# RWKV and attention in a hybrid encoder layer: side products moved to other places of TensorE's order, the value projection first, the queries' low part in both partition halves

## Chip, cores and metric

One core of a Trainium2 chip runs the whole layer. The metric is the device time of one execution in microseconds (us), lower is better. Time before: 884.14 us, the median of 3 runs (883.92 to 884.91).

## What is computed

One encoder layer on x of 512 positions by 1024 channels, float32. The parts that the change touches, from the reference:

```python
# h = rms_norm(x); proj = h @ w_in, its columns go to four mixers A, B, C, D and four gates
# B: stick-breaking attention, 4 heads x 64; mask is kpos < qpos
z = einsum('bhqd,bhkd->bhqk', qi, kh) * scale
log_beta = log_sigmoid(z)
log_keep = where(mask, log_beta - z, 0.0)
suffix = cumsum(log_keep, axis=3, reverse=True) - log_keep
attn = where(mask, exp(log_beta + suffix), 0.0)
out = einsum('bhqk,bhkd->bhqd', attn, vh)
# C: RWKV-7, 4 heads x 64: S_t = S_{t-1} diag(w_t) + (S_{t-1} a_t) b_t^T + v_t k_t^T ; y_t = S_t r_t
# D: u * (causal 128x128 mixing of layer_norm(v)), with u, v = split(gelu(z))
merged = sum over the branches of sigmoid(gate_i) * (y_i @ out_i);  x = x + merged @ w_o
# then rms_norm, the gated FFN with a width-3 convolution (2816 hidden), and a last rms_norm
```

## The kernel before

**Products.** Every large product is made of triples: `mm3` (lines 168 to 172) issues three matmuls of 512 columns, hi·hi, hi·lo and lo·hi, since each float32 operand is split into a part `hi` in the matmul type fp32r and a remainder `lo` (`split`, lines 99 to 101: ScalarE casts hi at L100, VectorE subtracts at L101; in all other helpers that split, the same two lines show). A weight arrives in pieces of 256 KB on SyncE's queue, is split into `whi` and `wlo`, and is used by four triples; seven such pieces are held.

**Order.** TensorE's order is written by hand: it runs in program order of the code. All other engines get their order from a scheduler, and each then executes strictly in its order. After each triple `mm3` calls `tick()` (line 159), which advances side threads by one: "norm", "rw" (first RWKV half, later attention), "rw1" (second RWKV half) and "sg" (mixer D's tail). A thread is a generator, and its `yield n` waits n triples. The numbers n are the constants `YA` to `YH`, `Y1` and `YS` (lines 33 to 35), and these place the side products between the triples.

**The RWKV half** (`rwkv_half`, j = 0 and 1, two heads each) goes, in TensorE's order: the gate product with `g2` (L434), sums over a head's channels by a matmul with a block of ones (L416, via `head_sum`), 64-row instances against masks, and a triangular solve. For the solve VectorE forms inverses of 16x16 blocks, which go out to DRAM and come back as `Dc`, and from that `Dm` (L541). `all_inst` (L552) issues 16 products of 64x64 as one group; `P1` (Dm by AoT) comes `YC` triples after `AkV`, `T32` and `TT` (L566, L568) one step later, and L578 reads `T32`. After that come `GT`, `pC`, `pY` (L612 to L625), and six steps of the state scan (L639 on TensorE, L640 and L641 on VectorE), `YS` triples apart. Between head sums and scan VectorE also computes the normalised keys (L462 and on) from `y0`, which ScalarE makes with a logarithm and an exponential (L448, L449).

**Mixer D's tail** (`sg_tail`): gelu of four 128x512 blocks on ScalarE (L794), layer-norm statistics and twelve operations on VectorE (L810 to L812, three for each block), the causal mixing on TensorE (L817).

**Attention.** Queries, keys and values come from three products of 16 triples each, in this order. Per head (four: `j`, `hp`), with `own` the head's 64 partitions and `oth` the other 64: `kS[:, hp]` holds k_hi on `own` and k_lo on `oth`; `qS[:, hp]` holds q_hi on both; `qL` holds q_lo on `own` only. The scores take, for each of four key blocks `si` (512, 384, 256 and 128 columns wide), one product over 128 rows (L931: k_hi·q_hi + k_lo·q_hi), one over 64 rows (L932: k_hi·q_lo) and the mask (L933). This is called the z block below. Then, 1 triple later, ScalarE takes |z|, an exponential and a logarithm (L940 to L942), VectorE adds (L944), a split gives `spH`, `spL`, and `YE` = 15 triples later L952 takes the cumulative sums; ScalarE takes the exponential (L956), a split gives `aH`, `aL`, and `YF` = 5 triples later L964 multiplies with the values. The values were transposed at L908, directly after their product. ScalarE also computes the branch gates (L850, a sigmoid); it loads a function table (ACT_TABLE_LOAD) where the next function isn't in the one that is loaded.

Of the kernel before, what the change touches and what calls it, by code (L numbers as in the profile page):

```python
# [9 lines left out]
F32 = mybir.dt.float32  # L10
F32R = mybir.dt.float32r
# [4 lines left out]
P = 128  # L16
# [13 lines left out]
NWB = 9  # L30
NACT = 8

YA, YB, YC, YD, YE, YF, YG, YH = 6, 16, 32, 20, 15, 5, 11, 3
Y1 = 3
YS = 2
WN = 19
WN2 = 5
ND = 3
# [10 lines left out]
def hybrid_encoder_layer(  # L49
# [22 lines left out]
    def bank(tag="mm"):  # L72
        return psum.tile([P, 512], F32, tag=tag, name=tag, bufs=4)
# [55 lines left out]
    def col_unit(w, *cols, get=piece):  # L129

        n = 256 // len(cols)
        return [get(2, [(slice(n * i, n * i + n), w[:, 2 * h:2 * h + 2, c:c + n]) for i, c in enumerate(cols)]) for h in range(w.shape[1] // 2)]
# [10 lines left out]
    def spawn(thread, gen):  # L143
        threads.setdefault(thread, []).append([gen, 0])
# [194 lines left out]
    def gemm2(u):  # L339

        ps = [bank(), bank()]
        for ci, kt in [(ci, kt) for h in range(4) for ci in range(2) for kt in range(2 * h, 2 * h + 2)]:
            hi, lo = u[kt // 2]
            cs = slice(ci * P, (ci + 1) * P)
            mm3(ps[ci], hi[:, kt % 2, cs], lo[:, kt % 2, cs], hH[:, kt, :], hL[:, kt, :], kt == 0, kt == KT - 1)
        return ps
# [50 lines left out]
    def rwkv_half(j, lora, xg, zk, zr, zv):  # L397
# [31 lines left out]
        cs = t2("tF", "cs")  # L429
        vec.tensor_tensor_scan(out=cs, data0=scan_m.rearrange("p c t -> p (c t)"), data1=sg, initial=0.0, op0=ALU.mult, op1=ALU.add)  # L430
        head_sum = parts_of(sq)
        yield 3
        pg = bank("wk")
        pe.matmul(pg, lhsT=g2[:, cj], rhs=xg, start=True, stop=True)  # L434
        gT = t2("gT", bufs=2)
# [435 lines left out]
    apool, ast = open_pool("apool", "right")  # L871


    HS = [slice(0, 64), slice(64, P)]
    qS, qL, kS, vS = [], [], [], []

    def lo_of(out, src, hi):
        vec.tensor_tensor(out=out, in0=src, in1=hi.bitcast(F32), op=ALU.subtract)

    pss2 = gemm2(col_unit(w_in_v, SB0))  # L880
    for j in range(2):
        ps = pss2[j]
        qs = apool.tile([P, 2, T], F32R, tag="qS", name="qS", bufs=2)
        ql = apool.tile([P, T], F32R, tag="qL", name="qL", bufs=2)
        for hp in range(2):
            own, oth = HS[hp], HS[1 - hp]
            act.mul(qs[own, hp, :], ps[own, :], 0.125)
            act.mul(qs[oth, hp, :], ps[own, :], 0.125)
            vec.scalar_tensor_tensor(out=ql[own, :], in0=ps[own, :], scalar=0.125, in1=qs[own, hp, :].bitcast(F32), op0=ALU.mult, op1=ALU.subtract)
        qS.append(qs)  # L890
        qL.append(ql)
    pss2 = gemm2(col_unit(w_in_v, SB0 + 256))
    for j in range(2):
# [4 lines left out]
            act.copy(ks[own, hp, :], ps[own, :])  # L898
            lo_of(ks[oth, hp, :], ps[own, :], ks[own, hp, :])
        kS.append(ks)  # L900
    pss2 = gemm2(col_unit(w_in_v, SB0 + 512))
    for j in range(2):
        ps = pss2[j]
        v = apool.tile([P, T], F32, tag="vT", name="vT", bufs=2)
        act.copy(v, ps)
        pt = bank("wk")
        for s in range(4):
            pe.transpose(out=pt[:, s * P:(s + 1) * P], in_=v[:, s * P:(s + 1) * P], identity=ident)  # L908
        vs = apool.tile([P, 2, NT, P], F32R, tag="vS", name="vS", bufs=2)
        for hp in range(2):  # L910
            own, oth = HS[hp], HS[1 - hp]
            src = pt.rearrange("p (s c) -> p s c", s=4)[:, :, own]
            act.copy(vs[:, hp, :, own], src)
            lo_of(vs[:, hp, :, oth], src, vs[:, hp, :, own])
        vS.append(vs)

    OFF = [0, 512, 1024, 896]
    W = [512, 384, 256, 128]
    def attention():
        for j in range(2):  # L920
            yt = apool.tile([P, T], F32, tag="yt", name="yt", bufs=2)
            for hp in range(2):
                own, oth = HS[hp], HS[1 - hp]
                zb = [bank("wk"), bank("wk"), bank("wk")]

                def zreg(si, t0=0):
                    b, o = divmod(OFF[si], 512)
                    return zb[b][:, o + t0:o + W[si]]

                for si in range(4):  # L930
                    pe.matmul(zreg(si), lhsT=kS[j][:, hp, si * P:(si + 1) * P], rhs=qS[j][:, hp, si * P:T], start=(si != 3), stop=False)  # L931
                    pe.matmul(zreg(si), lhsT=kS[j][own, hp, si * P:(si + 1) * P], rhs=qL[j][own, si * P:T], start=False, stop=False)  # L932
                    pe.matmul(zreg(si)[:, 0:P], lhsT=ident_r, rhs=neg_r, start=False, stop=(si != 1))  # L933
                yield Y1
                az = apool.tile([P, 1280], F32, tag="az", name="az", bufs=2)
                spH = apool.tile([P, 1280], F32R, tag="spH", name="spH", bufs=2)
                spL = apool.tile([P, 1280], F32R, tag="spL", name="spL", bufs=2)
                BR = [(0, 512, 512), (512, 1024, 512), (1024, 1280, 256)]
                for b, (a, e, w) in enumerate(BR):
                    act.activation(out=az[:, a:e], in_=zb[b][:, 0:w], func=AF.Abs)  # L940
                act.activation(out=az, in_=az, func=AF.Exp, scale=-1.0)
                act.activation(out=az, in_=az, func=AF.Ln, bias=1.0)  # L942
                for b, (a, e, w) in enumerate(BR):
                    vec.scalar_tensor_tensor(out=az[:, a:e], in0=zb[b][:, 0:w], scalar=0.0, in1=az[:, a:e], op0=ALU.max, op1=ALU.add)  # L944
                split(az, spH, spL)
                yield YE
                for si in range(4):
                    for sj in range(si, 4):
                        lt = tri_r if sj == si else mones_r
                        reg = zreg(si, (sj - si) * P)  # L950
                        for n, s_ in enumerate((spH, spL)):
                            pe.matmul(reg, lhsT=lt, rhs=s_[:, OFF[sj]:OFF[sj] + W[sj]], start=False, stop=(sj == 3 and n == 1), skip_group_check=True)  # L952
                aH = apool.tile([P, 1280], F32R, tag="spH", name="aH", bufs=2)
                aL = apool.tile([P, 1280], F32R, tag="spL", name="aL", bufs=2)
                for b, (a, e, w) in enumerate(BR):
                    act.activation(out=az[:, a:e], in_=zb[b][:, 0:w], func=AF.Exp)  # L956
                for a, e in ((0, 512), (512, 1280)):
                    split(az[:, a:e], aH[:, a:e], aL[:, a:e])
                yield YF
                po = bank("wk")  # L960
                for si in range(4):
                    cols = slice(OFF[si], OFF[si] + W[si])
                    for n, a_ in enumerate((aH, aL)):
                        pe.matmul(po[:, si * P:T], lhsT=vS[j][:, hp, si, :], rhs=a_[:, cols], start=(si == 0 and n == 0), stop=(si == 3 and n == 1))  # L964
                act.copy(yt[own, :], po[oth, :])
                vec.tensor_tensor(out=yt[own, :], in0=po[own, :], in1=yt[own, :], op=ALU.add)
            y_split("b", j, yt)
# [174 lines left out]
```

## Time and profile before

| | us |
|---|---|
| median of 3 runs | 884.14 (883.92 to 884.91) |
| the profiled execution, its own time | 885.09 |
| its span, first to last instruction | 883.4 |
| mean granted TensorE clock, of full speed | 0.992 |
| VectorE busy | 506.0 (57%) |
| ScalarE busy | 413.2 (47%) |
| GpSimd busy | 18.9 (2%) |
| DMA, mean rate | 93 GB/s |

The profile's page names engines PE (TensorE matmuls), PEld (TensorE weight loads), DVE (VectorE), ACT (ScalarE), POOL (GpSimd), SP (SyncE). An instruction is shown with the line of the code, the engine, the operation, output <- inputs, and a shape. Matmul ends are modelled by the profiler, and matmuls overlap, so what one costs is read as the distance from its start to the next start. In square brackets stands the idle time of the engine ahead of an instruction and what ended it.

### The profile page before, as it was taken

The page shows a single profiled execution, that of the slowest core. Times are in us where ns is not written, and L with a number is a line of the kernel's source. Part 1 is how long each engine was busy: PE and PEld are TensorE (multiplying, and loading weights), DVE is VectorE, ACT ScalarE, POOL GpSimd, SP SyncE. Part 2 cuts the span into 40 slices and gives each one's busy share as a digit, 9 for nine tenths or more (in the row PEclk, how much of TensorE's full clock was granted, in tenths as well). Part 3 has the DMA queues.
Part 4 walks back from the last instruction along what each step waited for, and adds up shares of the span by engine and source line. Part 5 has one row for each costly group of instructions (what it writes and reads, how often), then busy time and mean ns, then how long its engine had stood idle before and what let it go on. Part 6 is the DMA issues. An engine that isn't in the chain of part 4 may idle for free.

```text
span 883.4 us, 12631 instructions
## 1 busy us (share of the span) xinstructions
PE 865.9 (98%) x4767; PEld 709.8 (80%) x4767; DVE 506.0 (57%) x868; ACT 413.2 (47%) x676; POOL 18.9 (2%) x61
## 2 busy tenths in 40 slices
PE   6999999999999999999999999999999999999997
PEld 6978877788778788888888898888888888888876
DVE  5577747875364555544554676634665366634645
ACT  7473345643344587765344554413443144413425
POOL 6000000000000000000000000000000000000000
PEclk9999999999999999999999999999999999999999
DMA  7223331233133322226336252314432063314102
GB/s 242 63 83 99 86 97 49 63 87 97 52 86 93 99 62 65 73 62 200 96 96 182 69 167 96 96 37 117 134 96 84 8 183 107 96 37 131 36 1 95
DMA packets 102773, 82.20 MB, mean 93 GB/s; under 512 B 12716, under 2 KB 92152, under 8 KB 102712
## 3 DMA queue, kind: packets, MB, share of 16 engines
q1 hardware_dynamic: 102040, 79.82, 30.4%
q10 hardware_dynamic: 592, 1.31, 0.5%
q8 instruction: 37, 0.61, 0.3%
q0 software_dynamic: 80, 0.26, 0.1%
q14 instruction: 24, 0.20, 0.1%
HBM read 78.88 MB, written 2.49 MB: 92 GB/s over the span
## 4 chain that ended last, share of the span: by engine, by line
PE 87%; DMA 5%; DVE 4%; ACT 2%; issue 1%; SPq 1%; POOL 0%; ACTq 0%; DVEq 0%
PE mm L169 24%; PE mm L170 24%; PE mm L171 24%; PE wk L169 2%; PE wk L171 2%; PE wk L170 2%; PE wk L552 1%; PE wk L952 1%; DMA raw<-in_w_o_dram 1%; DMA raw<-in_w_in_dram 1%; DMA raw<-in_w_up_dram 1%; DVE wlo L101 1%; DMA x<-in_x_dram 1%; ACT whi L100 1%; PE wk L932 1%
## 5 line engine op out<-in xcount | busy, mean ns | idle before, releaser
L100 ACT CAST whi<-raw 128x512 fp32r<-128x512 f32 x276 | 169.1, 620 | 305.0 <-PE mm L170 148.3
L101 DVE TENSOR_TENSOR wlo<-raw,whi 128x512 fp32r<-128x512 f32 x272 | 185.4, 688 | 172.2 <-ACT whi L100 168.9
L169 PE MATMUL mm<-hH,whi 128*128 128x512 f32 (+1 forms) x448 | 174.3, 389 | 0.9 <-ACT hH L100 0.9
L171 PE MATMUL mm<-hH,wlo 128*128 128x512 f32 (+1 forms) x448 | 169.9, 379 | 3.6 <-POOL wlo L101 3.6
L170 PE MATMUL mm<-hL,whi 128*128 128x512 f32 (+1 forms) x448 | 169.7, 379 | 1.0 <-DVE hL L101 0.9
L170 PE MATMUL mm<-h2L,whi 128*128 128x512 f32 (+1 forms) x368 | 141.0, 383 | 0.5 <-DVE h2L L101 0.5
L169 PE MATMUL mm<-h2H,whi 128*128 128x512 f32 (+1 forms) x368 | 141.2, 384 | 0.1
L171 PE MATMUL mm<-h2H,wlo 128*128 128x512 f32 (+1 forms) x368 | 140.9, 383 | 0.0
L171 PEld LDWEIGHTS mm<-hH,wlo 128*128 128x128 f32 x448 | 85.9, 192 | 19.6 <-POOL wlo L101 3.8
L169 PEld LDWEIGHTS mm<-hH,whi 128*128 128x128 f32 x448 | 85.9, 192 | 18.2 <-issue 1.5
L170 PEld LDWEIGHTS mm<-hL,whi 128*128 128x128 f32 x448 | 85.9, 192 | 15.1 <-DVE hL L101 1.4
L170 PEld LDWEIGHTS mm<-h2L,whi 128*128 128x128 f32 x368 | 69.3, 188 | 14.8 <-DVE h2L L101 0.7
L169 PEld LDWEIGHTS mm<-h2H,whi 128*128 128x128 f32 x368 | 69.3, 188 | 14.5 <-ACT h2H L100 0.3
L171 PEld LDWEIGHTS mm<-h2H,wlo 128*128 128x128 f32 x368 | 69.3, 188 | 14.2
L171 PE MATMUL mm<-whi,aL 128*128 128x512 f32 (+1 forms) x92 | 35.8, 389 | 0.0
L169 PE MATMUL mm<-whi,aH 128*128 128x512 f32 (+1 forms) x92 | 35.7, 388 | 0.0
L170 PE MATMUL mm<-wlo,aH 128*128 128x512 f32 (+1 forms) x92 | 35.7, 388 | 0.0
L169 PE MATMUL wk<-whi,aH 128*128 128x512 f32 (+1 forms) x88 | 34.1, 388 | 0.0
L171 PE MATMUL wk<-whi,aL 128*128 128x512 f32 (+1 forms) x88 | 34.1, 387 | 0.0
L170 PE MATMUL wk<-wlo,aH 128*128 128x512 f32 (+1 forms) x88 | 34.1, 387 | 0.0
L1061 DVE SCALAR_TENSOR_TENSOR ga<-mm,vecs,ga 128x511 f32<-128x511 f32 x22 | 16.5, 749 | 26.4 <-ACT ga L1060 26.4
L1060 ACT ACTIVATE ga<-mm,vecs 128x512 f32<-128x512 f32 x22 | 15.1, 688 | 26.5 <-PE mm L171 26.5
(347 smaller groups left out, 1196.4 us busy)
## 6 DMA issues: line engine op xcount, KB each, us to landing
raw<-in_w_in_dram SPq DMA_DIRECT2D x104, 256.0 KB
raw<-in_w_up_dram SPq DMA_DIRECT2D x176, 128.0 KB
raw<-in_w_down_dram SPq DMA_DIRECT2D x44, 256.0 KB
raw<-in_w_o_dram SPq DMA_DIRECT2D x16, 256.0 KB
x<-in_x_dram SPq DMA_DIRECT2D x4, 512.0 KB
raw<-in_w_in_dram SPq DMA_DIRECT2D x16, 128.0 KB
xt<-in_x_dram SPq DMA_DIRECT2D x4, 512.0 KB
out_dram<-xn SPq DMA_DIRECT2D x4, 320.0 KB
```

What stands on the lines that cost most here:

```text
L100: act.copy(hi, src)
L101: eng.tensor_tensor(out=lo, in0=src, in1=hi.bitcast(F32), op=ALU.subtract)
L169: pe.matmul(ps, lhsT=sh, rhs=mh, start=first, stop=False)
L170: pe.matmul(ps, lhsT=sh, rhs=ml, start=False, stop=False)
L171: pe.matmul(ps, lhsT=sl, rhs=mh, start=False, stop=last)
L552: pe.matmul(ps[us, i * 64:i * 64 + 64], lhsT=lt, rhs=rh, start=True, stop=True)
L932: pe.matmul(zreg(si), lhsT=kS[j][own, hp, si * P:(si + 1) * P], rhs=qL[j][own, si * P:T], start=False, stop=False)
L952: pe.matmul(reg, lhsT=lt, rhs=s_[:, OFF[sj]:OFF[sj] + W[sj]], start=False, stop=(sj == 3 and n == 1), skip_group_check=True)
L1060: act.activation(out=t0, in_=ps, func=AF.Copy, scale=ffc(2, i))
L1061: vec.scalar_tensor_tensor(out=t0[:, 1:T], in0=ps[:, 0:T - 1], scalar=ffc(1, i), in1=t0[:, 1:T], op0=ALU.mult, op1=ALU.add)
```

## The change

1. `rwkv_half`: the wait ahead of L434/L416 is the constant `YN` = 5 where the number 3 stood: the product with `g2` and the first head sum come 2 triples later, and so does all that follows them in the thread.
2. `YC` goes from 32 to 36: `P1` and what follows it come 4 more triples later.
3. `YS` goes from 2 to 3: the steps of the state scan stand 3 triples apart.
4. The value projection stands ahead of those of queries and keys. Its transposes (after the change L897) and splits go into a thread "sg", `YV` = 4 triples after the product, beside the queries' product.
5. `attention` begins with a wait of `YK` = 7 triples.
6. `qL` is [P, 2, T], with q_lo of a head in both partition halves (four more 64x512 `scalar_tensor_tensor`), and L932 takes `kS[:, hp]` by `qL[:, hp]` over all 128 rows. This adds k_lo·q_lo to the scores.

```diff
-YA, YB, YC, YD, YE, YF, YG, YH = 6, 16, 32, 20, 15, 5, 11, 3
+YA, YB, YC, YD, YE, YF, YG, YH = 6, 16, 36, 20, 15, 5, 11, 3
 Y1 = 3
-YS = 2
+YS = 3
+YN = 5
+YV = 4
+YK = 7
...
         head_sum = parts_of(sq)
-        yield 3
+        yield YN
...
+    pss2 = gemm2(col_unit(w_in_v, SB0 + 512))
+    vT = []
+    for j in range(2):
+        v = apool.tile([P, T], F32, tag="vT", name="vT", bufs=2)
+        act.copy(v, pss2[j])
+        vT.append(v)
+
+    def turn_values():
+        yield YV
+        for j in range(2):
+            pt = bank("wk")
+            for s in range(4):
+                pe.transpose(out=pt[:, s * P:(s + 1) * P], in_=vT[j][:, s * P:(s + 1) * P], identity=ident)
...
+    spawn("sg", turn_values())
     pss2 = gemm2(col_unit(w_in_v, SB0))
...
-        ql = apool.tile([P, T], F32R, tag="qL", name="qL", bufs=2)
+        ql = apool.tile([P, 2, T], F32R, tag="qL", name="qL", bufs=2)
         for hp in range(2):
             own, oth = HS[hp], HS[1 - hp]
-            act.mul(qs[own, hp, :], ps[own, :], 0.125)
-            act.mul(qs[oth, hp, :], ps[own, :], 0.125)
-            vec.scalar_tensor_tensor(out=ql[own, :], in0=ps[own, :], scalar=0.125, in1=qs[own, hp, :].bitcast(F32), op0=ALU.mult, op1=ALU.subtract)
+            for to in (own, oth):
+                act.mul(qs[to, hp, :], ps[own, :], 0.125)
+                vec.scalar_tensor_tensor(out=ql[to, hp, :], in0=ps[own, :], scalar=0.125, in1=qs[own, hp, :].bitcast(F32), op0=ALU.mult, op1=ALU.subtract)
...
     def attention():
+        yield YK
...
-                    pe.matmul(zreg(si), lhsT=kS[j][own, hp, si * P:(si + 1) * P], rhs=qL[j][own, si * P:T], start=False, stop=False)
+                    pe.matmul(zreg(si), lhsT=kS[j][:, hp, si * P:(si + 1) * P], rhs=qL[j][:, hp, si * P:T], start=False, stop=False)
```

The order of the engines after the change comes from the scheduler. Lines of the changed kernel are 3 higher than before up to the gates (L566 is L569) and 12 higher in attention (L942 is L954); L101 is L104.

**VectorE where `T32` is formed.** L797 and L796 are layer-norm statistics of mixer D, L810 to L812 its twelve operations, and `T_1309` is `T32`. Before:

```order
L796 BN_STATS bst<-uv 128x6
L566 TENSOR_TENSOR T_1309<-wk,Dm 128x512
L797 BN_AGGR mv<-bst 128x2
L796 BN_STATS bst<-uv 128x6
L568 TENSOR_TENSOR TT<-wk,Dm 128x512
L797 BN_AGGR mv<-bst 128x2
L802 COPY wsT<-wk 128x512
L796 BN_STATS bst<-uv 128x6
L101 TENSOR_TENSOR wlo<-raw,whi 128x512
L797 BN_AGGR mv<-bst 128x2
L804 TENSOR_SCALAR lrstd<-mv 128x4
L807 RECIPROCAL lrst_1377<-lrstd 128x4
L810 TENSOR_SCALAR uv<-uv,mv,lrst_1377 128x256 x2
```

After (`T_1398` is `T32`):

```order
L807 TENSOR_SCALAR lrstd<-mv 128x4
L810 RECIPROCAL lrst_1320<-lrstd 128x4
L813 TENSOR_SCALAR uv<-uv,mv,lrst_1320 128x256 x2
L814 TENSOR_TENSOR uv<-uv,lngb 128x256 x2
L815 TENSOR_TENSOR uv<-uv,lngb 128x256 x2
L813 TENSOR_SCALAR uv<-uv,mv,lrst_1320 128x256 x2
L814 TENSOR_TENSOR uv<-uv,lngb 128x256 x2
L815 TENSOR_TENSOR uv<-uv,lngb 128x256 x2
L569 TENSOR_TENSOR T_1398<-wk,Dm 128x512
L571 TENSOR_TENSOR TT<-wk,Dm 128x512
L104 TENSOR_TENSOR wlo<-raw,whi 128x512 x2
```

`T32` and `TT` stood ahead of the twelve operations, and now stand behind them.

**VectorE in the second half of the state scan of j = 0.** L640 and L641 are a scan step's two operations; L462 takes `y_1763`, which is `y0` of half j = 1. Before:

```order
L640 SCALAR_TENSOR_TENSOR S<-S,wp 128x64
L477 TENSOR_TENSOR kbt<-k_1766,wm 128x4x2x64
L101 TENSOR_TENSOR qL<-rk,qH 128x512
L641 SCALAR_TENSOR_TENSOR S<-wk,wp,S 128x64
L640 SCALAR_TENSOR_TENSOR S<-S,wp 128x64
L101 TENSOR_TENSOR wlo<-raw,whi 128x512
L641 SCALAR_TENSOR_TENSOR S<-wk,wp,S 128x64
L462 SCALAR_TENSOR_TENSOR t_1839<-y_1763,ssm 128x512
L101 TENSOR_TENSOR wlo<-raw,whi 128x512
```

After (L643 and L644 are the step, L465 takes `y_1754`):

```order
L644 SCALAR_TENSOR_TENSOR S<-wk,wp,S 128x64
L104 TENSOR_TENSOR wlo<-raw,whi 128x512
L643 SCALAR_TENSOR_TENSOR S<-S,wp 128x64
L465 SCALAR_TENSOR_TENSOR t_1797<-y_1754,ssm 128x512
L644 SCALAR_TENSOR_TENSOR S<-wk,wp,S 128x64
L466 TENSOR_TENSOR t_1797<-t_1797,y_1754 128x512
L643 SCALAR_TENSOR_TENSOR S<-S,wp 128x64
L468 SCALAR_TENSOR_TENSOR kkn<-zk,vecs,y_1754 128x512
L104 TENSOR_TENSOR wlo<-raw,whi 128x512
L469 SCALAR_TENSOR_TENSOR kkn<-t_1797,kkn 128x512
L644 SCALAR_TENSOR_TENSOR S<-wk,wp,S 128x64
```

The operations on the second half's `y0` now stand between the scan's steps.

**ScalarE in attention, third and fourth head.** L940 to L942 make `az`, the L100 cast makes `spH`; L850 is a branch gate. Before, third head:

```order
L940 ACTIVATE az<-wk 128x512
L100 CAST whi<-raw 128x512
L941 ACTIVATE az<-az 128x1280
L942 ACT_TABLE_LOAD
L942 ACTIVATE az<-az 128x1280
L100 CAST whi<-raw 128x512
L850 ACT_TABLE_LOAD
L850 ACTIVATE gate<-mm,vecs 128x512
L100 CAST spH<-az 128x1280
L850 ACTIVATE gate<-mm,vecs 128x512
```

After, third head (L952 to L954, and L853 is the gate):

```order
L952 ACTIVATE az<-wk 128x512
L953 ACT_TABLE_LOAD
L953 ACTIVATE az<-az 128x1280
L853 ACT_TABLE_LOAD
L853 ACTIVATE gate<-mm,vecs 128x512
L954 ACT_TABLE_LOAD
L954 ACTIVATE az<-az 128x1280
L103 CAST whi<-raw 128x512 x4
L103 CAST spH<-az 128x1280
L103 CAST whi<-raw 128x512
```

After, fourth head, from the table of its last exponential on:

```order
L968 ACT_TABLE_LOAD
L968 ACTIVATE az<-wk 128x512
L968 ACTIVATE az<-wk 128x256
L103 CAST aH<-az 128x512
L968 ACTIVATE az<-wk 128x512
L853 ACT_TABLE_LOAD
L853 ACTIVATE gate<-mm,vecs 128x512
L103 CAST aH<-az 128x768
```

In the third head three table loads and a gate stand between |z| and `spH`, where one load stood ahead of the logarithm and one ahead of the gate; in the fourth a load and a gate stand ahead of the last cast `aH`, where before (not shown) that cast followed the exponential.

## Rows read from the trace of the kernel before

**Rows 1.** The page's part 1: busy us, share of the span, number of instructions.

```profile
PE 865.9 (98%) x4767; PEld 709.8 (80%) x4767; DVE 506.0 (57%) x868; ACT 413.2 (47%) x676; POOL 18.9 (2%) x61
```

**Rows 2.** The waits of PE: line, releaser, us in total, times, longest.

```profile
PE wk L908 <- ACT vT L905: 0.6, 1, 0.6
...
PE wk L639 <- DVE S L641: 0.5, 1, 0.5
```

**Rows 3.** The timeline of PE around `P1` of the first half: start, duration, instruction.

```profile
115.53 0.39 PE L171 MATMUL mm<-whi,hL 128*128 128x512 f32 x1
118.09 1.97 PE L552 MATMUL wk<-Dm,AoT 64*64 64x64 f32 x32 [2.17 <-DVE Dm L541]
...
121.40 0.39 PE L169 MATMUL mm<-whi,hH 128*128 128x512 f32 x1
```

**Rows 4.** The same around `P1` of the second half.

```profile
213.68 0.39 PE L171 MATMUL mm<-hH,wlo 128*128 128x512 f32 x1
...
215.88 0.39 PE L169 MATMUL mm<-y,whi 128*128 128x512 f32 x1
```

**Rows 5.** PE's waits at the line of the head sums.

```profile
  DVE qL L101: 1.0, 2
```

**Rows 6.** The timeline of PE at L817.

```profile
141.71 1.99 PE L817 MATMUL wk<-uv,wsT 128*128 128x256 f32 x8
143.35 0.58 PE L169 MATMUL mm<-hH,whi 128*128 128x512 f32 x1
```

**Rows 7.** The timeline of PE, first z block.

```profile
308.46 0.39 PE L931 MATMUL wk<-qS,kS 128*128 128x512 f32 x1
308.78 0.50 PE L932 MATMUL wk<-qL,kS 64*128 64x512 f32 x1
309.21 0.33 PE L933 MATMUL wk<-neg_r,ident_r 128*128 128x128 f32 x1
...
311.58 0.45 PE L169 MATMUL mm<-hH,whi 128*128 128x512 f32 x1
```

**Rows 8.** The timeline of PE, the cumulative sums of the first head.

```profile
323.97 0.39 PE L952 MATMUL wk<-spH,tri_r 128*128 128x512 f32 x1
324.20 0.39 PE L952 MATMUL wk<-spL,tri_r 128*128 128x512 f32 x1
...
326.67 0.44 PE L169 MATMUL mm<-y,whi 128*128 128x512 f32 x1
```

**Rows 9.** Windows: length, busy PE, PEld, DVE, ACT, POOL, granted clock, DMA share, GB/s.

```profile
381.00:384.00 3.00, 3.00 (x9) 2.33 (x8) 0.44 (x1) 2.73 (x4) 0.00 (x0) 0.50 0.00 0
```

**Rows 10.** The timelines of ACT (last gelu) and DVE (last of mixer D's twelve operations).

```profile
125.90 0.60 ACT L794 ACTIVATE uv<-mm 128x512 f32<-128x512 f32 x1 [2.31 <-PE mm L171]
...
133.81 0.75 DVE L812 TENSOR_TENSOR uv<-uv,lngb 128x256 f32<-128x256 f32 x2
```

**Rows 11.** The timelines of PE and ACT, from the second half's first head sum to `y0`.

```profile
155.00 0.50 PE L416 MATMUL wk<-qL,hones_r 128*128 128x512 f32 x1 [0.20 <-DVE qL L101]
...
161.36 0.63 ACT L449 ACTIVATE y<-y 128x512 f32<-128x512 f32 x1
161.90 0.60 ACT L100 CAST whi<-raw 128x512 fp32r<-128x512 f32 x1
```

**Rows 12.** Groups of instructions by line: busy us, mean ns of one, idle before them.

```profile
L850 ACT ACTIVATE gate<-mm,vecs 128x512 f32<-128x512 f32 x32 | 21.8, 687 | 8.7 <-PE mm L171 8.6
...
L850 ACT ACT_TABLE_LOAD x8 | 10.3, 1283 | 0.1
...
L101 DVE TENSOR_TENSOR spL<-az,spH 128x1280 fp32r<-128x1280 f32 x4 | 6.0, 1490 | 1.8 <-ACT spH L100 1.8
...
L942 ACT ACTIVATE az<-az 128x1280 f32<-128x1280 f32 x4 | 5.1, 1275 | 0.0
...
L100 ACT CAST spH<-az 128x1280 fp32r<-128x1280 f32 x4 | 5.0, 1262 | 2.5 <-DVE az L944 2.5
```

More of the change, by code (lines that the diff above doesn't have):

```diff
@@ L878, in lo_of @@
         vec.tensor_tensor(out=out, in0=src, in1=hi.bitcast(F32), op=ALU.subtract)
+    pss2 = gemm2(col_unit(w_in_v, SB0 + 512))
[10 more added lines that the diff above has]
+                pe.transpose(out=pt[:, s * P:(s + 1) * P], in_=vT[j][:, s * P:(s + 1) * P], identity=ident)
+            vs = apool.tile([P, 2, NT, P], F32R, tag="vS", name="vS", bufs=2)
+            for hp in range(2):
+                own, oth = HS[hp], HS[1 - hp]
+                src = pt.rearrange("p (s c) -> p s c", s=4)[:, :, own]
+                act.copy(vs[:, hp, :, own], src)
+                lo_of(vs[:, hp, :, oth], src, vs[:, hp, :, own])
+            vS.append(vs)
+    spawn("sg", turn_values())
     pss2 = gemm2(col_unit(w_in_v, SB0))
@@ L900, in hybrid_encoder_layer @@
         kS.append(ks)
[L901 to L915, printed above, removed]
     OFF = [0, 512, 1024, 896]
```

## Prediction

> **What bounds the kernel now.** I read the page's busy times first. TensorE is busy for 98% of the span, VectorE for 57%, ScalarE for 47% [rows 1], so the time is TensorE's stream of matmuls plus the places where that stream stops. The number of matmuls and their columns don't change, so I went to the waits of TensorE and to its timeline, and looked for places where the next start comes late. In the undisturbed stream a 512-column matmul starts 0.23 us after the one before it [rows 8], a triple every 0.69 us. That is the unit in which a delay "by n triples" is turned into time. Only distances between TensorE's starts go into the sum; an instruction added to VectorE or ScalarE costs nothing unless TensorE waits for it.
>
> **What the change can take away.**
>
> *`P1` later (`YC`, with `YN`).* In the first half, from the last matmul ahead of `P1` to the first matmul of the next triple but one, 5.87 us pass; the group waits 2.17 us for `Dm`, and the stream after it is slow [rows 3]. The same piece in the second half, with no wait, takes 2.20 us [rows 4]. If `Dm` is there, 3.67 us go. It came at about 118.0, just ahead of the group's start. Without the wait the group would have started 0.3 us after 115.53; now it comes 6 triples later (4 of `YC`, 2 of `YN`), 4.1 us, so at 119.9. `Dm` depends on products that `YN` moves by 2 triples, 1.4 us, so it comes at 119.4. The margin is 0.5 us, and what of it is missing would be the new wait. I take the whole -3.7.
>
> *Head sums later (`YN`).* Twice TensorE waits at L416 for the subtraction `qL`, 1.0 us in all [rows 5]. Two triples more, 1.4 us, are longer than either wait: -1.0.
>
> *L817.* Four products of 256 columns in two passes, 8 x 256 columns, are 0.9 us at 0.23 per 512; from its start to the next 1.64 pass [rows 6]. The products ahead of it on the same four banks are now another group. I take -0.7, with 0 as the other end.
>
> *State scan (`YS`).* One wait for `S`, 0.5 us [rows 2]: -0.5.
>
> *Transposes of the values.* They wait 0.6 us for the copy `vT` [rows 2]. With 4 triples between, 2.8 us, the wait goes: -0.6.
>
> *The z blocks.* The first takes 308.46 to 311.58, 3.12 us; the step from the 128-row product into the 64-row one is 0.32 and the one out of it 0.43, where 0.23 is normal [rows 7]. There are four blocks alike. How long does the block take with all rows 128? The cumulative sums are such a block: 5120 columns in 20 matmuls of the same mixed widths, 2.70 us, where 0.23 per 512 columns would give 2.30 [rows 8]. So it has 0.40 us for its four runs of widths. The z block has 3072 columns, 1.38 us, and with 0.40 it takes 1.8. That saves 1.3 each, -5.2 for the four; ends -4.8 and -6.0.
>
> The rule against this part is in the Trainium skill, page TensorEngine Tiling (Array Packing), section Overview: a contraction of 64 or fewer rows leaves the array underused, and its use in independent tiles can give up to 2x. By that, going from 64 to 128 rows spends a tile that could have worked beside another, and saves nothing: the sum would be -2.3 where it is -7.5. The same page (Key Properties) says that a change of tiling mode drains the engine, and that is nearer to the trace's 0.43 us step.
>
> *The clock after the fourth z block.* In the window 381 to 384 TensorE has a granted clock of 0.50, the 1.2 GHz level, right behind that block's waits and short products, and issues 9 matmuls in 3.0 us [rows 9]; at 0.23 they would take 2.1, so 0.9 us are lost. A block without slow steps may not be followed by it: I take -0.8, ends 0 and -1.6 (the fall may reach beyond the window).
>
> Gains: 3.7 + 1.0 + 0.7 + 0.5 + 0.6 + 5.2 + 0.8 = **12.5 us**.
>
> **What the change adds.** The orders of the engines show four places where an instruction that TensorE needs now stands behind another.
>
> *`T32` behind mixer D's twelve operations.* The last gelu ends at 126.5 before [rows 10]. `P1`'s stretch (5.87 less four matmuls, 5.0) and the two groups for `T32` and `TT` (2.0; one group is 2.20 less four matmuls, 1.3 [rows 4], and I take less in a pair) stood ahead of it and now follow it, so it ends near 119.6. The twelve operations end at 133.81 + 0.75 = 134.6, 8.1 after it [rows 10], so now at 127.7, and `T32` is done 0.8 to 1.3 later, at 128.5 to 129. TensorE reaches L578 at 119.9 + 1.3 (`P1`) + 6 triples (4.1) + 2.0 + some slow steps, 127.3 to 127.9. **+1.0**, ends 0 and +2.5.
>
> *The scan behind `y0`.* From the second half's first head sum (155.00) to `y0`'s end (161.36 + 0.63) 7.0 us pass, on ScalarE with its table loads [rows 11]. Now that sum is at triple 182, and the third scan step's L641 stands behind L462, which reads `y0`. So the step ends some 8.0 us after the sum (7.0, L462 of 512 columns 0.6 by `spL`'s 1.49 for 1280 [rows 12], and two small operations); TensorE wants its result at triple 189, 7 triples and about 1 us of side products later, 5.8. Two weight casts less on ScalarE would make it 6.9. **+1.5**, ends 0 and +2.5.
>
> *Third head's `spH`, `spL`.* In ScalarE's order now stand |z| (1.28, as any 1280 columns), the exponential and the logarithm (2.55), three table loads (3.85), a gate (0.69), five casts of 512 columns (0.60 each, 3.0) and `spH` (1.26), and then VectorE's `spL` (1.49): together 14.1 [rows 11, 12]. Neighbours on ScalarE overlap by 0.09 (161.90 against 161.36 + 0.63 [rows 11]), which leaves 13.2 to 13.7. TensorE comes after 18 triples, 12.4 to 12.7. **+1.0**, ends 0 and +2.5.
>
> *Fourth head's `aH`.* A load (1.28) and a gate (0.69) now stand ahead of its last cast [rows 12], 2.0 us on a chain that TensorE reaches 5 triples later. **+1.5**, ends 0 and +2.0.
>
> Costs: 1.0 + 1.5 + 1.0 + 1.5 = **+5.0 us**.
>
> **Edits at no cost.** The four more operations for `qL`, 0.6 us each by `spL`'s row [rows 12], 2.4 us on VectorE, are covered by the 16 triples (11 us) of the keys' product; without that cover they would delay the first z block by up to 2.4. The shift of attention by `YK` is covered by the triples of branch C's gates: its last product comes with the last of these, so that a later one would stand uncovered, about 0.5 us. The second RWKV half, which comes up to 23 triples later, ends ahead of attention's pools. Weight loads keep their number and bytes, with the queue's order changed by one column unit.
>
> **The sum.** -12.5 + 5.0 = -7.5. The profiled execution took 885.09, so 877.6; the median of the runs is 0.95 below it, so **876.6 us**. With no new wait, full clock and longest z saving it is 884.1 - 14.1 = 870.0; with the costs at 9.5, the z saving at 4.8 and neither clock nor L817, 884.1 - 10.6 + 9.5 = 883.0.
>
> **Rivals.**
>
> *A. The new waits don't appear*: each is a small difference of long chains, and the chains shorten where TensorE's waits ahead of them go. Then -12.5: 871.6. Against: all four would have to come out at their lower ends together. 0.27.
>
> *B. The 64 rows aren't the cause of the slow steps.* Then the z term is 0 and the sum -2.3: 881.8. Against it stands the 0.23 between equal all-128 rows [rows 8]. 0.07.
>
> *C. Slower: table loads cost twice their row.* ScalarE loads 39 tables where it loaded 34, and in attention 12 of them stand on the chains between z and `aL`. If each took 1.28 us more than its own row, that is 15.4 us, less 2.8 of slack, +12.6 on the sum -7.5: 889.2. It turns the sign from 0.9 us of extra time a load ((7.5 + 2.8) / 12). Against it: the idle time ahead of L850's functions is put down to TensorE for 8.6 of its 8.7 us in 32, and to no load [rows 12]. 0.03. The Trainium skill, page ScalarE: Activation LUTs, section What ACT_TABLE_LOAD costs, gives about 1283 ns for the load, as the rows have it, and 1380 ns of drain beside it, 2.66 us for a switch; by that the sum would be near rival C's.
>
> *D. The new waits are about twice their size.* +5.0 more or so, with the clock lost as before: near 883, within 0.2%. 0.06.
>
> **How the numbers follow.** My forecast has 0.57. The range of 8 in 10 goes from 870.0, below rival A by the largest z saving and the full clock, to 881.8, rival B; it leaves out C, D and the ends where all costs or all savings meet. A measurement of this kernel can tell 0.2%, 1.8 us, from no change. Faster by more: forecast, A and B, 0.91; within: D, 0.06; slower: C, 0.03.
>
> **What would show it.** `P1` starting with no wait for `Dm`: right for the largest wait. z blocks at about 1.8 us: right; still 3.1: B. Granted clock in the window behind the fourth block. Waits of TensorE for `T32` (at L578's place), for `S` in the first scan, for `spL` in the third head and `aL` in the fourth, of 1 to 1.5 us each: right; none: A. ScalarE idle behind table loads: C. Wrong altogether if TensorE waits more than 10 us in new places or the last attention product stands bare behind the gates of C.

## The result, and the profile after

The changed kernel takes **873.69 us** (median of 4 runs, 873.64 to 874.94) against 884.52 (883.92 to 885.52) for the kernel before on the same chip: a ratio of 0.988, 95% interval 0.9863 to 0.9897. Forecast were 876.6 and a range of 870.0 to 881.8. The profiled execution took 873.64, with a span of 871.9 us where it was 883.4.

The page's part 1, after. It answers to [rows 1]:

```profile
PE 857.9 (98%) x4767; PEld 706.7 (81%) x4767; DVE 509.7 (58%) x872; ACT 418.7 (48%) x681; POOL 18.9 (2%) x61
```

The matmuls are as many as before, and TensorE is busy 8 us less: most of the gain lies in steps that were counted as busy. The four more DVE operations and the five more ACT instructions (table loads) are there.

The waits of PE after, those that the change concerns (line, releaser, us in total, times, longest). They answer to [rows 2, 5]:

```profile
PE wk L976 <- DVE aL L104: 0.8, 1, 0.8
PE wk L581 <- DVE T L569: 0.6, 1, 0.6
PE wk L964 <- DVE spL L104: 0.5, 1, 0.5
...
PE wk L642 <- DVE S L644: 0.3, 1, 0.3
```

The waits for `Dm`, `vT` and the old one for `S` are gone. In their place stand four waits, at the four places that the prediction named, and each is shorter than forecast.

The timeline of PE after, `P1` of the first half, L820 (the L817 of before), and the first z block. These answer to [rows 3, 6, 7]:

```profile
118.90 0.40 PE L174 MATMUL mm<-hH,wlo 128*128 128x512 f32 x1
119.23 1.15 PE L555 MATMUL wk<-Dm,AoT 64*64 64x64 f32 x32
120.31 0.50 PE L172 MATMUL mm<-hH,whi 128*128 128x512 f32 x1
...
131.01 1.99 PE L820 MATMUL wk<-uv,wsT 128*128 128x256 f32 x8
132.65 0.58 PE L172 MATMUL mm<-hH,whi 128*128 128x512 f32 x1
...
307.10 0.39 PE L943 MATMUL wk<-qS,kS 128*128 128x512 f32 x1
307.33 0.39 PE L944 MATMUL wk<-qL,kS 128*128 128x512 f32 x1
307.56 0.22 PE L945 MATMUL wk<-neg_r,ident_r 128*128 128x128 f32 x1
...
308.75 0.45 PE L172 MATMUL mm<-hH,whi 128*128 128x512 f32 x1
```

`P1` starts 0.33 us after the last matmul, with no wait. L820 takes 1.64 us, as before. The z block takes 1.65 us where it took 3.12, and the step out of the second product is 0.23 where it was 0.43.

**Where the time went, by stages.** The two kernels issue the same 1156 triples in the same number, so the start of a triple with the same number marks the same amount of main work. The lengths of the stages, from the timelines of PE (us; triples 17 to 130 hold the first RWKV half up to `AkV`, 130 to 200 the solve, the scan and mixer D's tail, 324 to 466 the values' transposes and attention):

| stage, triples | before | after | difference |
|---|---|---|---|
| start to 17 | 25.59 | 24.48 | -1.11 |
| 17 to 130 | 72.49 | 72.42 | -0.07 |
| 130 to 200 | 74.10 | 69.85 | -4.25 |
| 200 to 324 | 106.71 | 106.69 | -0.02 |
| 324 to 466 | 129.45 | 123.81 | -5.64 |
| 466 to 640 | 114.73 | 114.38 | -0.35 |
| 640 to 1155 | 353.86 | 353.87 | 0.01 |

The first stage holds nothing that the change touches. Over the kernels of this study it took 24.4 to 25.8 us, 25.59 and 24.63 in two executions of the kernel before, so its 1.1 us are chance. The same holds for triples 466 to 640 (114.4 to 115.1). The first stage's length goes with the clock: in the four profiles with 25.3 to 25.8 us (before, the first of experiment 2, experiments 3 and 9) the granted clock stays at 0.50 for one stretch of 6.8 us towards its end, in the ten with 24.4 to 24.8 us for shorter ones.

What differs in the stages that the change touches is the -4.25 and the -5.64: **-9.9 us** in this pair of profiles. Some 1.6 us of each is a stretch at 1.2 GHz that the profile of before has and the one of after has not. The repeat of the kernel before (experiment 11) has only the second of them, and against it the two stages give -2.64 and -5.64, 8.3 us.

### The profile page after: what moved, and what is told of

It reads as the page before. It is cut to its first block, busy times and chain, and to the rows that moved or that the text cites. A ratio compares the mean times of both kernels' runs of the same rounds, so it can differ in the third digit from the quotient of the medians.

```text
span 871.9 us, 12631 instructions
## 1 busy us (share of the span) xinstructions
PE 857.9 (98%) x4767; PEld 706.7 (81%) x4767; DVE 509.7 (58%) x872; ACT 418.7 (48%) x681; POOL 18.9 (2%) x61
## 4 chain that ended last, share of the span: by engine, by line
PE 92%; DVE 2%; ACT 2%; DMA 2%; issue 1%; SPq 1%; POOL 0%; ACTq 0%; POOLq 0%
PE mm L172 25%; PE mm L174 25%; PE mm L173 25%; PE wk L174 3%; PE wk L172 3%; PE wk L173 3%; PE wk L555 1%; PE wk L964 1%; DMA x<-in_x_dram 1%; DMA raw<-in_w_up_dram 1%; PE wk L976 1%; PE wk L499 1%; DVE wlo L104 0%; PE wk L525 0%; DMA raw<-in_w_in_dram 0%
## 5 line engine op out<-in xcount | busy, mean ns | idle before, releaser
L104 DVE TENSOR_TENSOR wlo<-raw,whi 128x512 fp32r<-128x512 f32 x272 | 184.9, 688 | 167.4 <-ACT whi L103 162.5
```

The lines of the kernel that those rows point to most:

```text
L104: eng.tensor_tensor(out=lo, in0=src, in1=hi.bitcast(F32), op=ALU.subtract)
```

## Experiments

All compare with the kernel before on the same chip. A length of a stage is that of the table above.

**1. The low part alone.** The kernel before with part 6.

```diff
-ql = apool.tile([P, T], F32R, tag="qL", name="qL", bufs=2)
+ql = apool.tile([P, 2, T], F32R, tag="qL", name="qL", bufs=2)
...
-rhs=qL[j][own, si * P:T]
+rhs=qL[j][:, hp, si * P:T]
```

> The kernel before with part 6 of the change alone (q_lo in both halves, the second score product over 128 rows). Theory, the 64-row steps cost their mode: every z block takes 1.65 to 1.8 us instead of 3.12 to 3.17, -5.4 to -5.8 us, and the low clock behind the fourth block (window 381 to 384 of before) goes with it, another -1.6: 876.7 to 877.1 on a before of 884.1. Rival, the low clock belongs to the place of the fourth head among branch C's gates and not to the block: it is still seen at 1.2 GHz there, and the time is 878.3 to 878.7.

Measured: 876.19 us against 884.01, ratio 0.9911 (0.989 to 0.9932). The first z block takes 1.65 us instead of 3.12, and each of the three others, with the products ahead of it, 2.93 or 2.94 instead of 4.38 or 4.39: 5.8 us less in all. In this profile the clock falls behind none of them, and the stage 324 to 466 is 122.44 instead of 129.45. This one edit is most of the change's gain. No head waits for `spL` or `aL` here.

**2. All but the low part.** The changed kernel with part 6 taken back, in two executions.

```diff
-pe.matmul(zreg(si), lhsT=kS[j][:, hp, si * P:(si + 1) * P], rhs=qL[j][:, hp, si * P:T], ...)
+pe.matmul(zreg(si), lhsT=kS[j][own, hp, si * P:(si + 1) * P], rhs=qL[j][own, si * P:T], ...)
```

> The changed kernel with part 6 taken back (q_lo in one half, 64 rows). Theory: z blocks of 3.1 us again, +5.8 us on the changed kernel, 879.5; if the slow blocks also bring back the low clock behind one of them, +7.4, 881.1. Rival, the new waits for spL and aL come from the shorter z blocks: they go here, and the time is 2.1 lower, 877.4.

Measured: 880.8 us against 884.01, ratio 0.9961 (0.9946 to 0.9976). The stage 324 to 466 takes 129.33, 5.5 more than in the changed kernel, with no low clock in that profile. The waits for `aL` (0.8) and `spL` (0.2, where the changed kernel has 0.5) are still there, so the rival fell: the short blocks don't make them, though that for `spL` is longer with them. The kernel was profiled once more:

> The changed kernel with part 6 taken back, once more, for a second profile. Theory: with interleaved 64-row products a low clock behind a z block can come here too (none in its first profile); about 3 in 4. Rival: it never comes with these places, and the block's slow steps have no part in it.

That execution (882.51) has two stretches at the lower clock, behind the first and behind the third z block. Windows of it (length, busy PE, PEld, DVE, ACT, POOL, granted clock, DMA share, GB/s):

```profile
310.00:314.00 4.00, 4.00 (x12) 3.16 (x12) 0.00 (x0) 3.53 (x4) 0.00 (x0) 0.58 0.18 58
358.00:362.00 4.00, 4.00 (x12) 3.14 (x13) 0.69 (x1) 3.95 (x5) 0.00 (x0) 0.57 0.00 0
```

TensorE is shown without idle time in either and issues 12 matmuls in 4 us instead of 17: 1.2 GHz for most of the window. Each costs some 1.5 us, and this stage is 132.12, 2.8 more than in the other execution. So one kernel loses its clock nowhere or twice.

**3. The RWKV places alone.** The kernel before with parts 1 to 3.

```diff
-YC = 32; YS = 2; yield 3
+YC = 36; YS = 3; yield 5
```

> The kernel before with parts 1 to 3 alone (YN 5, YC 36, YS 3). Theory: the wait for Dm goes (-3.7), a wait for T32 of 0.6 and one for S of 0.3 come, the second half's head sum saves 0.46 and the first nothing, in all -3.2 to -3.8: 880.3 to 880.9. Rival, the RWKV places matter only together with the later attention (weights, VectorE): less than 1.5 us, over 882.6. The low clock behind the fourth z block should stay in either.

Measured: 881.6 us against 884.01, ratio 0.9977 (0.9962 to 0.9993). That is 2.4 us less, short of the theory's 3.2 to 3.8 and above the rival's 1.5. The stage 130 to 200 takes 69.84, as in the changed kernel, so the RWKV places don't need the later attention; `T32` (0.6) and `S` (0.3) are waited for. Against the 74.10 of the first profile of before that is 4.3 less, against the 72.49 of its repeat (experiment 11) 2.65: the theory took the wait for `Dm` at its length in an execution that lost the clock there. The low clock of attention came behind the third z block here, not the fourth.

**4. Values first and the later attention alone.** The kernel before with parts 4 and 5.

```diff
+pss2 = gemm2(col_unit(w_in_v, SB0 + 512))
+spawn("sg", turn_values())
...
 def attention():
+    yield YK
```

> The kernel before with parts 4 and 5 alone (values first, attention 7 triples later), 64-row products as before. Theory: the values' transposes take 0.79 instead of 1.59 us (-0.8); waits for spL in the third and aL in the fourth head, if ScalarE's order with a load and a gate in the chain comes from the 7 triples, +2.1: 885.4. Rival, that order comes from the short z blocks: no such waits, -0.8, 883.3. If the low clock depends on where the fourth head stands, 1.6 less in either case.

Measured: 883.7 us against 884.01, ratio 1.0 (0.9981 to 1.0019). The transposes save 0.8; the wait for `aL` (0.8 by the list of waits) is there with 64-row blocks, and that for `spL` is 0.2. The stage 324 to 466 is 130.74, 1.3 more than before, as the theory had it, with one stretch of low clock in both. The median doesn't tell the two apart: 883.7 lies nearer the rival's 883.3 than the theory's 885.4, and the ten runs go from 881.51 to 887.86. The waits do: the order of ScalarE comes from the later attention. These two parts by themselves bring nothing that can be measured: the later heads pay for the transposes.

**5. The z block regrouped.** The kernel before; four 128-row products, then four 64-row products, then four masks.

```diff
-for si in range(4): hi product; 64-row product; mask
+for si in range(4): hi product
+for si in range(4): 64-row product
+for si in range(4): mask
```

> The kernel before with the z block's products in another order: four 128-row products, then the four 64-row products, then the four masks; rows, columns and number as before. Theory, the loss is at the steps from 128 to 64 rows and back (0.39 us for each of four pairs): one pair is left, the block takes 1.65 + 0.4 = 2.0 to 2.1 us instead of 3.12, -4.2 us for four blocks. Rival, a 64-row product is itself slower: the block still takes about 3.1 us and nothing is saved.

Measured: 877.79 us against 883.7, ratio 0.9937 (0.9918 to 0.9957). The timeline of PE of this kernel, first block:

```profile
305.77 0.56 PE L931 MATMUL wk<-qS,kS 128*128 128x512 f32 x2
306.57 0.42 PE L931 MATMUL wk<-qS,kS 128*128 128x256 f32 x2 [0.24 <-DVE vS L878]
306.92 0.85 PE L933 MATMUL wk<-qL,kS 64*128 64x512 f32 x4
307.69 0.66 PE L935 MATMUL wk<-neg_r,ident_r 128*128 128x128 f32 x4
308.19 0.45 PE L169 MATMUL mm<-hH,whi 128*128 128x512 f32 x1
```

The block takes 2.42 us, 0.24 of it a wait, where 2.0 to 2.1 were expected, and the four 64-row products take 0.77 us for 1280 columns, which at 0.23 per 512 is 0.58 and a step of 0.2: the products themselves are not slower than with 128 rows. The later blocks save 1.14 to 1.17 each of the 1.45 that full width saves, so the one pair of steps that is left costs 0.3; the four blocks together take 4.2 us less. So the loss is in the steps between 64 and 128 rows, not in the 64-row products; with four pairs and 1.45 to 1.47 us lost in a block it is some 0.37 us a pair. The rival fell. The clock didn't fall in this profile; one of the seven runs, 882.68 us at a mean granted clock of 0.991 where the other six have 0.995 to 0.997, shows that it can fall in this kernel too.

**6 to 8. The new waits taken back.** The changed kernel with `P1` 2 triples earlier, with attention 5 triples earlier, and with both.

```diff
-YC = 36        -YK = 7
+YC = 34        +YK = 2
```

> The changed kernel with YC 34 instead of 36; in VectorE's order T32 then stands ahead of mixer D's twelve operations, TT still behind them. Theory: P1 comes 2 triples earlier, 0.5 us behind Dm, so that wait stays away; the wait for T32 (0.57, with what follows it 0.73) goes: -0.7 us on the changed kernel, 873.0. Rival: TT is now what is late, and the product after L578 waits for it, or Dm does: 0 or slower.

> The changed kernel with YK 2 instead of 7. ScalarE's order in the last step of the fourth head then has no load and gate ahead of the last cast aH, and in the third head one load less ahead of spH; the fourth head has a load and a gate between exponential and logarithm. Theory: the wait for aL (with what follows, 1.35) goes and that for spL moves to the fourth head at up to 0.8: -1.3 to -2.1 us on the changed kernel, 871.6 to 872.4. Rival: keys aren't ready 5 triples earlier and the first z block waits 1 us or more: no gain.

> The changed kernel with YC 34 and YK 2. Theory: both savings add, -2.0 to -2.8 us on the changed kernel, 870.9 to 871.7. Rival: the two orders of VectorE and ScalarE shift each other and one wait comes back: as the better of the two alone.

Measured: 873.34 (ratio 0.9878, 0.9861 to 0.9896), 874.0 (0.9886, 0.9867 to 0.9904) and 872.64 (0.9874, 0.985 to 0.9897), each against 883.7. They lie 0.3 us above the expected 873.0, 1.6 above 871.6 to 872.4 and 0.9 above 870.9 to 871.7, and from the changed kernel's 873.69, measured in other runs, they differ by no more than its own runs do among themselves. So the stages have to speak. With `YC` 34 the wait for `T32` is gone and with it that for `S`, which the theory didn't name; the stage 130 to 200 takes 69.12, 0.73 less for both. That `T32` was late by the order on VectorE is borne out. With `YK` 2 the waits for `aL` and `spL` are gone, but two waits for a gate stand in their place, 1.2 us with what follows them:

```profile
PE mm L172 <- ACT gate L853: 0.9, 2, 0.5
```

That row is from the waits of PE of the eighth kernel, and the seventh has the same. The stage 324 to 466 falls by 0.9 (to 122.92) and 1.0, not by 2.1. The two waits stand ahead of the first two heads' cumulative sums, at a product of the main stream that writes a bank `mm`; by the profile it is released when a gate, which reads such a bank, is done.

**9 and 10. Attention earlier still.** `YC` 34, and `YK` 1 or no wait.

```diff
-YK = 2        -yield YK
+YK = 1
```

> The changed kernel with YC 34 and YK 1. Theory: ScalarE's order in the first two heads now has the gates behind spH and fewer casts behind, so the two waits of TensorE for a gate (0.63 and 0.57 with YK 2) shrink to half or less; no wait for aL or spL; keys ready just in time: -0.6 us on the kernel with YC 34 and YK 2, 872.0. Rival: the first z block waits for kS about as much as is saved, no difference.

> The changed kernel with YC 34 and no wait at attention's start. ScalarE's order is then that of the first experiment, in which no head waited. Theory: no waits for gates, spL or aL, one wait of up to 1 us for kS ahead of the first z block: -0.5 to -1.2 us on the kernel with YC 34 and YK 2, 871.4 to 872.1. Rival: the wait for kS is over 1.2 us, no gain.

Measured: **871.8 us** (871.44 to 872.31; 884.5 before; ratio 0.986, 0.9843 to 0.9878) and 872.92 (0.9877, 0.9855 to 0.9899). The waits of PE of the ninth kernel are all of them such as the change doesn't touch:

```profile
PE mm L174 <- POOL wlo L104: 3.5, 1, 3.5
PE wk L227 <- DVE ones_f L83: 1.3, 1, 1.3
PE mm L290 <- DVE diag L285: 0.9, 1, 0.9
PE mm L173 <- DVE hL L104: 0.9, 1, 0.9
PE mm L172 <- ACT hH L103: 0.9, 1, 0.9
PE mm L173 <- DVE h2L L104: 0.5, 1, 0.5
PE mm L172 <- ACT h2H L103: 0.3, 1, 0.3
```

Its stages 130 to 200 and 324 to 466 take 69.12 and 121.39, together 3.15 us less than in the changed kernel. The two profiled executions differ by 1.5 (872.14 against 873.64), since this one's first stage is 25.58, 1.1 longer, and its triples 466 to 640 take 0.45 more; the medians differ by 1.9. With no wait at all attention takes 122.07: an `aL` (0.4 with its restart) and a gate (0.4) are late again. The wait for `kS` that I expected in the tenth, and had as the rival in the ninth, did not come; the ninth is within 0.2 us of its 872.0, the tenth misses its 871.4 to 872.1.

**11. The kernel before, profiled again.**

> The kernel before, once more, for a second profile. Theory: the low clock behind a z block comes in some executions and not in others; whether here, and behind which block, isn't foreseen (about 3 in 4 by the profiles with interleaved 64-row products so far). Rival: it is a fixed part of this kernel, and comes again behind the fourth block, 1.6 us.

Measured: 882.33 us in one run. The low clock came again behind the fourth block, as the rival has it; that it isn't fixed is shown by the two executions of experiment 2, not by this one. Another stretch did not come. Windows behind the wait for `Dm`, first in the profile of before that the prediction used, then here:

```profile
118.00:122.00 4.00, 3.91 (x38) 3.48 (x39) 1.15 (x2) 1.87 (x3) 0.00 (x0) 0.58 0.26 75
```

```profile
117.00:121.00 4.00, 4.00 (x65) 3.27 (x67) 1.34 (x3) 2.87 (x5) 0.00 (x0) 1.00 0.25 66
```

In the first the engine is busy but at 1.2 GHz for most of the window; in the second it has full speed, and the stage 130 to 200 takes 72.49 instead of 74.10.

## Why the prediction held, step by step

| step of the sum | forecast | measured | by |
|---|---|---|---|
| wait for `Dm` | -3.7 | -3.7 in this pair of profiles; -2.1 where the clock holds | [rows 3, 4], experiment 11 |
| head sums | -1.0 | -0.5 | 1.79 to 1.33 in the second half; 1.32 both times in the first |
| L817 | -0.7 | 0 | 1.64 both times |
| old wait for `S` | -0.5 | -0.6 | step of 0.94 us at 157.63, 0.33 without a wait |
| values' transposes | -0.6 | -0.8 | 1.59 to 0.79 |
| z blocks | -5.2 | -5.8 | 3.12 to 1.65, then 1.45 a block |
| low clock behind the z blocks | -0.8 | -1.6 in this pair | experiments 1, 2, 11 |
| `T32` | +1.0 | +0.6 | 126.53 to 127.49, 0.96; the same step took 0.33 before |
| scan behind `y0` | +1.5 | +0.3 | step of 0.64 us at 158.88, 0.33 without a wait |
| third head's `spL` | +1.0 | +0.8 | block of 3.52 instead of 2.72 |
| fourth head's `aL` | +1.5 | +1.4 | block of 2.57 instead of 1.22 |

**The z blocks** were right in cause and near in size: the cumulative sums were the right block to read the price from. Experiment 5 settles that it is the change of rows, as the Trainium skill's page TensorEngine Tiling (Array Packing), Key Properties, has it for a change of tiling mode; that page gives no price, and here it is 0.3 to 0.37 us for a pair of steps. The rule of its Overview, by which 128 rows would spend an array that could have been shared, would, as it is applied in the prediction, have given a sum of -2.3; the stages show -9.9, or -8.3 against the repeat.

**The new waits** came where the orders of the engines said, all four: rival A, that none appears, is wrong. The rows around `T32` after, VectorE and then TensorE:

```profile
126.08 0.76 DVE L815 TENSOR_TENSOR uv<-uv,lngb 128x256 f32<-128x256 f32 x2
126.75 0.69 DVE L569 TENSOR_TENSOR T<-wk,Dm 128x512 f32<-128x512 f32 x1
```

```profile
127.49 0.69 PE L581 MATMUL wk<-T,MT 32*32 32x32 f32 x32 [0.57 <-DVE T L569]
```

`T32` starts as the twelfth operation of mixer D ends. I had the operations end at 127.7, and they end at 126.8. The third head's product waits for `spL`; for it the prediction counted five casts ahead of `spH`, where ScalarE's order shows four (2.17 us in the trace for the 3.0 taken).

```profile
365.57 0.50 PE L964 MATMUL wk<-spL,tri_r 128*128 128x512 f32 x1 [0.53 <-DVE spL L104]
```

The fourth head, on ScalarE, then on TensorE:

```profile
391.10 1.28 ACT L853 ACT_TABLE_LOAD   x1
392.39 0.69 ACT L853 ACTIVATE gate<-mm,vecs 128x512 f32<-128x512 f32 x1
392.98 0.82 ACT L103 CAST aH<-az 128x768 fp32r<-128x768 f32 x1
```

```profile
395.12 0.44 PE L976 MATMUL wk<-aL,vS 128*128 128x384 f32 x1 [0.82 <-DVE aL L104]
```

The load and the gate delay the last cast by 1.9 us (2.0 were worked out), and TensorE loses 1.35 of it. The gate starts at 392.39, where the load of 1.28 us that began at 391.10 ends: a load costs its own row here and nothing beside it, so rival C is wrong too. So are B, with blocks of 1.65 us, and D: the four waits cost 3.1 us and not about 10. (D's own terms add up to 882.4, not to near 883.)

**The scan** is the term that was mis-sized most, 1.5 for 0.3. The step was "the step ends some 8.0 us after the sum", taken from a distance of 7.0 in a stretch where ScalarE had more in front of `y0`. After the change:

```profile
155.06 0.63 ACT L452 ACTIVATE y<-y 128x512 f32<-128x512 f32 x1
```

```profile
155.72 0.69 DVE L465 SCALAR_TENSOR_TENSOR t<-y,ssm 128x512 f32<-128x512 f32 x1 [1.06 <-ACT y L452]
156.33 0.28 DVE L644 SCALAR_TENSOR_TENSOR S<-wk,wp,S 128x64 f32<-128x64 f32 x1
```

From the same head sum (150.11) to `y0`'s end it is 5.6 us, not 7.0. VectorE did stand 1.06 us for `y0`, but S was ready by 156.61, in time for TensorE's next product at 156.67. The wait of 0.25 us comes one step later, where the next L644 (159.19) stands behind four 512-column operations.

**Two terms were no waits, or only in part.** The first half's head sum takes 1.32 us before and after, although its data now come 2 triples earlier: its 0.63 us step behind the product with `g2` isn't idle time for `qL`. I took the 1.0 us of [rows 5] for a delay of TensorE's matmuls, and it is the sum over the line's instructions, weight loads too, of which 0.46 us showed in the stream. And L817's 1.64 us stayed when another group of small products came ahead of it. In experiments 6, 8, 9 and 10, where a triple stands there, it takes 1.54. So the wait for banks that I supposed is not shown anywhere; what makes its eight products slow wasn't tried.

**The clock** was half chance. I set half of a stretch's loss because I didn't know whether it belongs to the block. Six profiles of this study have 64-row products between 128-row ones: before, its repeat, experiments 2 (twice), 3 and 4. They show six stretches of low clock in attention, right behind a first, third or fourth block; one profile has none and one has two. The seven profiles with full rows (after, experiments 1 and 6 to 10) and the regrouped one have none. Each of the six begins within 0.1 to 0.4 us of a block's end. That the interleaved blocks bring it about is likely by this count, and not shown beyond it; in which execution it comes isn't to be told. The mean granted clocks of all runs fit: the ten of experiment 4, whose kernel has the wait for `Dm` too, go from 881.51 us at 0.996 to 887.86 at 0.988, while the 24 of the changed kernel and experiments 6 to 10 have 0.993 to 0.997. The Trainium skill, page TensorE: Matmul & The Clock Gate, What's actually happening, says of the rise at a kernel's start that the same kernel has another number of slow matmuls from run to run. Here a fall in the midst of the kernel varies in the same way: 72.49 and 74.10 us for the same stage of the same kernel.

The `Dm` term of -3.7 held in size by chance. 1.6 us of the 5.87 were not the wait: they were a stretch at 1.2 GHz behind it, which the prediction read only as a slow stream. Two of the five profiles with that wait have it (before and experiment 1), three have not (experiments 4, 5 and 11); without it the term is -2.1.

So the sum of -7.5 was some 2.4 short of the stages' -9.9: costs 3.1 instead of 5.0 (1.9), z, transposes and the old wait for `S` 0.9, the clock 0.8, against head sums and L817, 1.2 too much. The rest of the 11.5 us between the two spans is mostly the start's chance (1.1). The z blocks and the four waits were forecast by their causes; of the size, some 3.2 us are the two stretches of low clock that this execution of before happened to have.

## What to carry to other kernels

Where TensorE is busy 98% of the time, look for steps that are longer than the columns make them, not only for idle time: a 64-row product between 128-row ones cost some 0.37 us for the pair of steps, and filling the rows, or grouping the 64-row products, gave back 5.8 or 4.2 us with no product fewer. When products are moved, read the new order of the other engines for what now stands ahead of their inputs, a table load and a gate, or twelve operations of another branch; each of the four places so named was a real wait, of 0.3 to 1.4 us, and moves of two and of six triples took them away again, while one triple more brought `aL` and a gate back. And compare stages by equal work before you believe a median: 1.1 us of the first stage and 1.6 us for each stretch of low clock came and went between executions of one kernel.

## What the runs showed that I had not expected

A wait costs TensorE more than its line in the list says: `aL`'s 0.82 us made 1.35 in the stream, `spL`'s 0.53 made 0.80 and `T32`'s 0.57 made 0.63. A 512-column matmul is shown with 0.39 us while the next starts after 0.23, so between two of these the idle time counted from its end leaves 0.16 us out, and the first step after a wait is longer too (0.34 us instead of 0.23 behind `spL`'s, 0.28 instead of 0.17 behind `aL`'s). A wait can also be missing from the list: in the changed kernel the triple that starts at 317.28 comes 0.44 us after the matmul ahead of it, and the next matmul 0.34 after that, at a place where experiments 7 and 8 list a wait for a gate.

The lower clock came in a stream that is shown with no idle time at all: the engine was busy for 4.00 of 4.00 us in each of the windows of experiment 2 (ends of matmuls are modelled), and what preceded it was a z block with 64-row steps.
